# Attention transposes, key copies and mLSTM transposes moved, and the order of all queues made with a timeline simulation

## The chip, the cores and the metric

The kernel runs on one core of one Trainium2 chip. The metric is device time in microseconds (us) of one execution; the profile is of one execution on the same core. TensorE (PE) multiplies and transposes, VectorE (DVE) and ScalarE (ACT) do elementwise work, GpSimd (POOL) a small part of it, and SyncE (SP) issues nearly all transfers (DMA). Each engine works through a queue of its own, and engines wait for each other by semaphores.

## The reference

Two layers of an encoder are applied to 768 tokens: a sequence of 256 (token tiles 0 and 1, of 128 tokens each) and one of 512 (tiles 2 to 5). Weights are shared. All data is float32. Cut to what matters:

```
for l in range(2):
    aq, ak, av, lq, lk, lv, lo, lg = split(x @ w_in[l])
    att  = rmsnorm(diff_attention(aq, ak, av))        # 4 heads: softmax(s0) - lam * softmax(s1), with a distance bias
    h    = mlstm(lq, lk, lv, lg) + reversed mlstm     # 4 heads, in chunks of 128 tokens, states carried between them
    lstm = sigmoid(lo) * rmsnorm(h)
    x = layer_norm(ALPHA * x + concat(att, lstm) @ w_out[l])
    gate, up = split(x @ w_gu[l])                     # 2 x 2816 columns
    x = layer_norm(ALPHA * x + (gelu(conv3(gate)) * up) @ w_down[l])
```

## The kernel before

Every large product is made of three passes over float32r operands: a value is split into a high part and a rest (`wh` and `wl` for weights, the two halves of `actA` and `actB` for activations), and high x high, high x rest and rest x high are summed in PSUM. The class `Weights` loads each weight block by a DMA on SP into one of six `raw` buffers, and converts it: ACT writes `wh` (L171), DVE writes `wl` (L172). Twelve converted blocks may wait for use. For the FFN, DVE and POOL also form differences of blocks, T1 to T4 (L149), since the gate and up products are made by a scheme of seven products in place of eight.

A layer runs in these stages:

- The mLSTM's inputs and gates, and the values `av` and `lv` (`dense`, `lstm_in`, `gates`).
- Attention by heads: `att_in(h)` makes queries and keys (tiles aqkA, aqkB) and copies the keys into `sK` with their rest in `kL`; `att(h)` goes over the two sequences and their query tiles. For one query tile it makes two scores s (L728, L729), reduces them on DVE (L730), takes exponentials on ACT, combines the two halves on DVE (L737), transposes the result on PE (aT, L740), and multiplies with the values (u, L744). At a sequence's end `ao` is the normalised output, and PE transposes it (aoT, L757).
- The mLSTM by six chunks, `lstm_out(c)`: queries and keys are transposed (qkT, L592; copies into `qz` and `kt`), kq is their product (L615), DVE weighs it with the decay `pt` (L618) and the queries with `qet` (L622), PE makes the numerators num of four heads (L633, L636), and DVE and ACT divide and normalise them in `hq` (den, L643 to L656). `qet` has one buffer, and a DMA fills it for the next chunk (L602). `lo` (L345) is a dense product, its gate is applied to `hq`.
- W_out (tiles wo, L898), by two halves of the columns and six token tiles. In the second half each token tile is normalised (`layer_norm`, L845 to L857), sums S1 to S4 are formed on POOL or DVE (`combine`, L880 to L883), and PE transposes them (tiles y0T and y1T, L362), which ACT and DVE split into `actA` and `actB` (L364, L365).
- The FFN: 22 column tiles of seven products p (L942), and the down product dn by groups of three or four of these (L1002), added to `acc` on DVE (L1009).

Eight PSUM banks are shared by tags: three for d (dense tiles), two for s, one each for t, u and L. A tile that needs a bank waits until the tile before it in the bank was read.

The order in which the code is written isn't the order on the engines. `weave` mixes generators by shares, `prio` shifts the priority of what is issued inside it, and the framework's scheduler then sets the order of each engine's queue, by readiness in a simulation of its own and by priority. Only the order in each queue is fixed; on the chip an instruction at the head of a queue waits for its semaphores, and everything behind it waits with it. Chunks and heads meet in two lines:

```
weave((chain(att_in(1), att(1)), AT1, PR_A), (chain(lstm_states(lc), *[lstm_out(lc, c) for c in range(OUTS)]), 4 * OUTS + 9, PR_L), ...)
weave((chain(att_in(2), att(2)), AT2, PR_A), (chain(*[lstm_out(lc, c) for c in range(OUTS, NT)]), 4 * (NT - OUTS) + 1, PR_L), ...)
```

Names of tiles below carry numbers: s, aT and u have head, first token tile and query tile (s2200: head 2, sequence from tile 2, query tile 0, softmax half 0), kq and qkT the chunk, num chunk and head, lo and wo the token tile, raw, wh and wl the block.

## Time and profile before

| | us |
|---|---|
| Median of 3 runs | 1815.83 |
| Lowest and highest run | 1812.57 and 1816.02 |
| The profiled execution | 1814.85 |
| Its span, first to last instruction | 1813.1 |
| PE busy in the span | 1772.2 |
| DVE busy | 1348.4 |
| ACT busy | 774.3 |
| POOL busy | 244.4 |

An engine counts as busy while a record of it lasts. PE's matmuls overlap, so a busy PE may still wait for short times; how far apart matmuls start tells more. The granted clock of TensorE was 0.998 of full speed over the execution. The first matmul starts 7.3 us after the span's start, and the last 8.1 us are layer norm and output of the last token tile.

### The profile page before, as it was taken

To read this page: it belongs to the slowest core of one execution; us is meant where nothing else is said; L and a number is where in the kernel's file an instruction comes from. 1 tells how busy PE (TensorE), PEld (TensorE's weight loads), DVE (VectorE), ACT (ScalarE), POOL (GpSimd) and SP (SyncE) were. 2 spreads that over 40 slices of the span, in tenths; PEclk is the share of its full clock that TensorE was granted. 3 is DMA by queue.
4 is the path that set the end of the run, shared out by engine and by line. 5 is a ranking of instruction groups with operands and counts; after the bars stand their busy time and mean duration, and the time that the engine had idled before them with its cause. 6 is when DMAs were issued, how large, how long until landed. Compare 5 with 4: busy or idle time off the path is not lost. (4 is left out here: it accounts for less than half of the span.)

```text
span 1813.1 us, 26263 instructions
## 1 busy us (share of the span) xinstructions
PE 1772.2 (98%) x9692; PEld 1575.5 (87%) x9692; DVE 1348.4 (74%) x2592; ACT 774.3 (43%) x1636; POOL 244.4 (13%) x266
## 2 busy tenths in 40 slices
PE   8999999999999999999999999999999999999998
PEld 8877887889889889899898778878899898898996
DVE  4546887599877787787955468876997787787778
ACT  4445667144334334344233556671453343343340
POOL 2001011141111111110110011101411110111102
PEclk9999999999999999999999999999999999999999
DMA  5312221303122122123232123122122221221211
GB/s 190 100 53 71 76 60 59 139 24 95 57 82 82 47 82 73 56 69 96 94 97 80 53 64 94 47 86 107 37 87 70 65 82 51 78 82 47 82 65 70
DMA packets 89232, 138.09 MB, mean 76 GB/s; under 512 B 7792, under 2 KB 33008, under 8 KB 89104
## 3 DMA queue, kind: packets, MB, share of 16 engines
q1 hardware_dynamic: 88384, 136.05, 23.7%
q8 instruction: 76, 1.25, 0.3%
q14 instruction: 52, 0.43, 0.1%
q10 hardware_dynamic: 720, 0.37, 0.1%
HBM read 130.00 MB, written 6.39 MB: 75 GB/s over the span
## 5 line engine op out<-in xcount | busy, mean ns | idle before, releaser
L942 PE MATMUL p<-actA,wh 128*128 128x384 f32 x1408 | 363.5, 338 | 3.2 <-DVE g L967 3.2
L171 ACT ACTIVATE wh<-raw 128x512 fp32r<-128x512 f32 (+1 forms) x348 | 215.8, 631 | 275.3 <-PE p L942 110.1
L172 DVE TENSOR_TENSOR wl<-raw,wh 128x512 fp32r<-128x512 f32 (+1 forms) x348 | 244.0, 712 | 62.2 <-ACT wh L171 61.7
L942 PE MATMUL p<-actB,wh 128*128 128x384 f32 x1056 | 270.1, 337 | 0.0
L942 PEld LDWEIGHTS p<-actA,wh 128*128 128x128 f32 x1408 | 254.7, 188 | 5.8 <-DVE g L967 3.8
L942 PE MATMUL p<-actA,wl 128*128 128x384 f32 x704 | 237.3, 337 | 0.0
L149 POOL TENSOR_TENSOR T<-raw,raw 128x512 f32<-128x512 f32 x88 | 120.3, 1370 | 837.4 <-DVE wl L172 483.9
L1002 PE MATMUL dn<-wh,actB 128*128 128x512 f32 x576 | 209.1, 396 | 1.4 <-DVE acc L1009 1.4
L171 ACT ACTIVATE wh<-T 128x512 fp32r<-128x512 f32 x176 | 108.5, 629 | 220.6 <-DVE acc L1009 105.3
L942 PEld LDWEIGHTS p<-actB,wh 128*128 128x128 f32 x1056 | 191.2, 188 | 0.0
L1002 PE MATMUL dn<-wh,ring 128*128 128x512 f32 x480 | 179.2, 397 | 1.6 <-DVE acc L1009 1.6
L942 PE MATMUL p<-actB,wl 128*128 128x384 f32 x528 | 177.2, 336 | 0.0
L1009 DVE TENSOR_TENSOR acc<-acc,dn 128x512 f32<-128x512 f32 x144 | 98.3, 683 | 72.2 <-PE dn L1002 72.0
L172 DVE TENSOR_TENSOR wl<-T,wh 128x512 fp32r<-128x512 f32 x176 | 129.8, 749 | 22.1 <-ACT wh L171 22.0
L1002 PEld LDWEIGHTS dn<-wh,actB 128*128 128x128 f32 x576 | 108.0, 188 | 30.3 <-DVE acc L1009 3.4
L942 PEld LDWEIGHTS p<-actA,wl 128*128 128x128 f32 x704 | 132.2, 188 | 0.1
L898 PE MATMUL wo<-wh,actB 128*128 128x512 f32 x384 | 122.9, 397 | 0.0
L1002 PE MATMUL dn<-wl,actB 128*128 128x512 f32 x288 | 113.2, 393 | 0.0
L1002 PEld LDWEIGHTS dn<-wh,ring 128*128 128x128 f32 x480 | 90.0, 188 | 24.6 <-DVE acc L1009 4.2
L942 PEld LDWEIGHTS p<-actB,wl 128*128 128x128 f32 x528 | 99.1, 188 | 0.0
L1002 PE MATMUL dn<-wl,ring 128*128 128x512 f32 x240 | 94.7, 395 | 0.0
L898 PEld LDWEIGHTS wo<-wh,actB 128*128 128x128 f32 x384 | 71.8, 188 | 16.2
(270 smaller groups left out, 3387.9 us busy)
## 6 DMA issues: line engine op xcount, KB each, us to landing
raw<-in_w_g_dram SPq DMA_DIRECT2D x88, 256.0 KB, 2.8
raw<-in_w_u_dram SPq DMA_DIRECT2D x88, 256.0 KB, 2.6
raw<-in_w_down_dram SPq DMA_DIRECT2D x88, 256.0 KB, 2.7
raw<-in_w_out_dram SPq DMA_DIRECT2D x32, 256.0 KB, 2.7
pt<-scr_m SPq DMA_DIRECT2D x12, 512.0 KB, 3.9
qet<-scr_e SPq DMA_DIRECT2D x12, 512.0 KB, 5.2
raw<-in_w_c_dram SPq DMA_DIRECT2D x16, 264.0 KB, 4.0
raw<-in_w_av_dram SPq DMA_DIRECT2D x16, 256.0 KB, 3.5
```

Source lines behind the costliest of these rows:

```text
L149: src["engine"].tensor_tensor(out=src["tile"], in0=a, in1=b, op=ALU.subtract)
L171: self.nc.scalar.activation(h, v, AF.Identity)
L172: self.nc.vector.tensor_tensor(out=l, in0=v, in1=h.bitcast(F32), op=ALU.subtract)
L898: PE.matmul(p, actB[:, k, a, t * 128:(t + 1) * 128], units[k][1 + b], start=n + i == 0, stop=n == 7 and i == 2)
L942: PE.matmul(ps, blk[1 + a][:, k * 128:(k + 1) * 128], x[:, k, b, :], start=k + i == 0, stop=k == 3 and i == 2)
L1002: PE.matmul(p, x, (wh_, wl_)[b], start=k + i == 0, stop=k == nf - 1 and i == 2)
L1009: V.tensor_tensor(out=z, in0=z, in1=p, op=ALU.add)
```

## The change

Four edits by hand and one switch:

- aoT, the transposes of a head's output, become a function `finish` that is put into a list; the list is worked off by `finish_sequence` behind the next unit's scores, or behind the next head's key product.
- The key copies are issued in the order in which the scores read them, and with priority 60.
- `lstm_qk` for the next chunk is called behind the numerators of the chunk, no longer ahead of them.
- `PR_AO` goes, and the bank of u is taken later.
- `schedule_with_timeline_sim=True`: the framework's scheduler uses its timeline simulation when it orders the queues.

```
--- before.py
+++ after.py
@@ -52,7 +52,6 @@
 PR_S = -20
 PR_T = -20
 PR_E = 50
-PR_AO = -40
 PR_CONV1 = -100
 PR_CONV2 = -100
 SBUFS = 2
@@ -84,6 +83,7 @@
 WO_K = (4,5,0,1,6,7,2,3)
 WO_ORDER0 = (0, 1, 2, 3, 4, 5)
 NSG = 3
+PR_K = 60
 AT1 = 11
 AT2 = 8
 AT3 = 12
@@ -620,8 +620,6 @@
             dirs = [di for di in range(2) if (di, c) in cst]
             for di in dirs:
                 EN[E_QE].tensor_tensor(out=qet[:, di], in0=qz.rearrange("p h r j -> p r h j"), in1=qet[:, di], op=ALU.mult)
-            if c + 1 < NT:
-                lstm_qk(lc, c + 1)
             yield
             pns = {}
             for h in range(4):
@@ -649,6 +647,8 @@
                 S.activation(pt[:, 0, h, :], hs, AF.Square, accum_out=ssq[:, c, h:h + 1])
                 if h % 2:
                     yield
+            if c + 1 < NT:
+                lstm_qk(lc, c + 1)
             G.tensor_scalar(rsl[:, c], ssq[:, c], 128 * EPS, 1.0, op0=ALU.add, op1=ALU.mult)
             G.tensor_tensor(out=rsl[:, c], in0=rsl[:, c], in1=mhalf[:, 0:4], op=ALU.pow)
             for h in range(4):
@@ -692,6 +692,7 @@
                 pA = P("d", f"aqkA{h}{ui}")
                 pBu = pB[:, ui * 256:(ui + 1) * 256]
                 feat_major(uu, pA, pBu)
+                finish_sequence()
                 W.done(*uu)
                 for ps, tk in ((pBu, slice(0, SB)), (pA, slice(SB, T))):
                     if ui == 0:
@@ -700,14 +701,21 @@
                         V.scalar_tensor_tensor(out=sQ[hi_, 0, tk], in0=ps[lo_], scalar=qs, in1=sQ[lo_, 0, tk].bitcast(F32), op0=ALU.mult, op1=ALU.subtract)
                         V.scalar_tensor_tensor(out=sQ[lo_, 1, tk], in0=ps[hi_], scalar=qs, in1=sQ[hi_, 1, tk].bitcast(F32), op0=ALU.mult, op1=ALU.subtract)
                     else:
-                        S.copy(sK[lo_, 0, tk], ps[lo_])
-                        S.copy(sK[hi_, 1, tk], ps[hi_])
-                        S.copy(sK[hi_, 0, tk], ps[lo_])
-                        S.copy(sK[lo_, 1, tk], ps[hi_])
-                        V.tensor_tensor(out=kL[lo_, 0, tk], in0=ps[lo_], in1=sK[lo_, 0, tk].bitcast(F32), op=ALU.subtract)
-                        V.tensor_tensor(out=kL[hi_, 1, tk], in0=ps[hi_], in1=sK[hi_, 1, tk].bitcast(F32), op=ALU.subtract)
+                        with prio(PR_K):
+                            S.copy(sK[lo_, 0, tk], ps[lo_])
+                            V.tensor_tensor(out=kL[lo_, 0, tk], in0=ps[lo_], in1=sK[lo_, 0, tk].bitcast(F32), op=ALU.subtract)
+                            S.copy(sK[hi_, 0, tk], ps[lo_])
+                            S.copy(sK[hi_, 1, tk], ps[hi_])
+                            V.tensor_tensor(out=kL[hi_, 1, tk], in0=ps[hi_], in1=sK[hi_, 1, tk].bitcast(F32), op=ALU.subtract)
+                            S.copy(sK[lo_, 1, tk], ps[hi_])
                 yield
 
+
+        pending = []
+
+        def finish_sequence():
+            while pending:
+                pending.pop(0)()
 
         def att(h):
             slope = 2.0 ** (-8.0 * (h + 1) / 4)
@@ -715,7 +723,7 @@
                 nq = s1 - s0
                 n = nq * 128
                 keys = slice(s0 * 128, s1 * 128)
-                pu = P("u", f"u{h}{s0}")
+                pu = None
                 ssu = sm.tile([128, 4], F32, tag="ssu", name=f"ssu{h}{s0}")
                 sm0 = sm.tile([128, 4], F32, tag="sm0", name=f"sm0{h}{s0}")
                 for qt in range(nq):
@@ -735,6 +743,9 @@
                     V.reciprocal(cc, cc)
                     V.scalar_tensor_tensor(out=cc, in0=sm0[:, qt:qt + 1], scalar=nlam[:, l:l + 1], in1=cc, op0=ALU.mult, op1=ALU.mult)
                     V.scalar_tensor_tensor(out=tp[:, 0, :n], in0=tp[:, 1, :n], scalar=cc, in1=tp[:, 0, :n], op0=ALU.mult, op1=ALU.add)
+                    if pu is None:
+                        finish_sequence()
+                        pu = P("u", f"u{h}{s0}")
                     pa = P(TAG_AT[qt % 2], f"aT{h}{s0}{qt}")
                     for st in range(nq):
                         PE.transpose(pa[:, st * 128:(st + 1) * 128], tp[:, 0, st * 128:(st + 1) * 128], ident)
@@ -751,11 +762,14 @@
                 ao = ra.tile([128, 512], F32, tag="aT", name=f"ao{h}{s0}", bufs=2)
                 V.tensor_tensor(out=ao[:, :n].rearrange("p (a b) -> p a b", b=128), in0=pu[:, :n].rearrange("p (a b) -> p a b", b=128),
                                 in1=ssu[:, :nq].unsqueeze(2).to_broadcast([128, nq, 128]), op=ALU.mult)
-                pt_ = P(TAG_AOT, f"aoT{h}{s0}")
-                with prio(PR_AO):
+
+                def finish(h=h, s0=s0, s1=s1, nq=nq, n=n, ao=ao):
+                    pt_ = P(TAG_AOT, f"aoT{h}{s0}")
                     for qt in range(nq):
                         PE.transpose(pt_[:, qt * 128:(qt + 1) * 128], ao[:, qt * 128:(qt + 1) * 128], ident)
-                S.activation(av[:, s0:s1, h * 128:(h + 1) * 128], pt_[:, :n].rearrange("p (a b) -> p a b", b=128), AF.Identity, scale=again[:, l, h:h + 1])
+                    S.activation(av[:, s0:s1, h * 128:(h + 1) * 128], pt_[:, :n].rearrange("p (a b) -> p a b", b=128), AF.Identity, scale=again[:, l, h:h + 1])
+
+                pending.append(finish)
 
         def weave(*gens):
 
@@ -811,6 +825,7 @@
             next(lo, None)
 
         weave((chain(att_in(3), att(3)), AT3, PR_A), (split_lstm(), 13 - L1 - L2, PR_LO), (chain(*[split_att(h) for h in range(3)]), 4))
+        finish_sequence()
         weave((split_att(3), 1))
         RA.close()
 
@@ -1105,7 +1120,7 @@
     d["scr_m"] = nc.dram_tensor("scr_m", (DEPTH, 8, T), F32, kind="Internal").ap()
     d["scr_e"] = nc.dram_tensor("scr_e", (DEPTH, 8, T), F32, kind="Internal").ap()
     d["scr_x"] = nc.dram_tensor("scr_x", (T, D), F32, kind="Internal").ap()
-    with tile.TileContext(nc) as tc:
+    with tile.TileContext(nc, schedule_with_timeline_sim=True) as tc:
         with ExitStack() as ctx:
             trunk(ctx, nc, tc, d, o, depth)
     return nc
```

No instruction that computes is added or removed. What the order of the queues becomes is seen in the built programs. In each pair of excerpts the first is of the kernel before.

PE, in the mLSTM chunks of the first layer, from chunk 3's product kq3 on. The tiles lo2 are dense work.

```order
L615 MATMUL kq3_2386<-qz_1847,kt3_2185 128x128 x3
L744 MATMUL u20_2347<-av_227,aT200_2369 128x128 x2
L740 MATMUL aT201_2420<-ident_214,tp201_2404 128x128 x2
L728 MATMUL s2201_2536<-sK_229,sQ_228 128x512
L729 MATMUL s2201_2536<-kL_230,sQ_228 128x512
L345 MATMUL lo2_2693<-wh49_1462,actA_70 128x512
L345 MATMUL lo2_2693<-wl49_1463,actA_70 128x512
L345 MATMUL lo2_2693<-wh49_1462,actA_70 128x512
L345 MATMUL lo2_2693<-wh50_1468,actA_70 128x512
L345 MATMUL lo2_2693<-wl50_1469,actA_70 128x512
L345 MATMUL lo2_2693<-wh50_1468,actA_70 128x512
L345 MATMUL lo2_2693<-wh51_1474,actA_70 128x512
```

```order
L615 MATMUL kq3_2386<-qz_1847,kt3_2337 128x128 x4
L755 MATMUL u20_2365<-av_227,aT200_2369 128x128 x2
L751 MATMUL aT201_2411<-ident_214,tp201_2395 128x128 x2
L736 MATMUL s2210_2581<-sK_229,sQ_228 128x512
L737 MATMUL s2210_2581<-kL_230,sQ_228 128x512
L736 MATMUL s2211_2585<-sK_229,sQ_228 128x512
L737 MATMUL s2211_2585<-kL_230,sQ_228 128x512
L631 MATMUL num30_2419<-cst30_1665,qet3_2316 128x129
L631 MATMUL num30_2419<-cst31_1744,qet3_2316 128x129
L634 MATMUL num30_2419<-vaug_237,pt3_2084 128x129 x2
L755 MATMUL u20_2365<-av_227,aT201_2414 128x128 x2
L631 MATMUL num31_2420<-cst30_1665,qet3_2316 128x129
```

In the kernel before, ten more matmuls of lo2 and the transposes qkT4 follow before num30. In the changed one lo0 to lo4 stand ahead of these rows, num30 comes seven rows after kq3, and up to kq5 only the 24 matmuls of lo5 are dense work.

DVE, at the end of W_out in the first layer: layer norm of token tile 4 (`acc` with mva04 and rsa04), the splits of transposes into `actA` and `actB`, and conversions wl of FFN weights.

```order
L851 SCALAR_TENSOR_TENSOR acc_3376<-acc_3376,mva04_3800,lng_3386 128x1024
L365 TENSOR_TENSOR actB_2834<-y0T32_3829,actB_2834 128x4x128
L857 SCALAR_TENSOR_TENSOR acc_3376<-acc_3376,rsa04_3801,lnb_3387 128x1024
L365 TENSOR_TENSOR actB_2834<-y0T33_3836,actB_2834 128x4x128
L365 TENSOR_TENSOR actA_70<-y0T34_3843,actA_70 128x4x128
L172 TENSOR_TENSOR wl81_3948<-T4_81_3945,wh81_3947 128x512
L172 TENSOR_TENSOR wl82_3956<-T2_81_3943,wh82_3955 128x512
L901 SCALAR_TENSOR_TENSOR acc_3376<-acc_3376,wo15_3850 128x512
```

```order
L866 SCALAR_TENSOR_TENSOR acc_3376<-acc_3376,mva04_3800,lng_3386 128x1024
L172 TENSOR_TENSOR wl81_3948<-T4_81_3945,wh81_3947 128x512
L172 TENSOR_TENSOR wl82_3956<-T2_81_3943,wh82_3955 128x512
L172 TENSOR_TENSOR wl83_3962<-T3_83_3959,wh83_3961 128x512
L172 TENSOR_TENSOR wl84_3966<-T1_81_3941,wh84_3965 128x512
L872 SCALAR_TENSOR_TENSOR acc_3376<-acc_3376,rsa04_3801,lnb_3387 128x1024
L172 TENSOR_TENSOR wl85_3970<-raw82_3583,wh85_3969 128x512
L916 SCALAR_TENSOR_TENSOR acc_3376<-acc_3376,wo15_3850 128x512
```

Four conversions now stand between the two steps of the layer norm of tile 4, and the splits of y0T33 and y0T34 come behind the step that reads wo15.

POOL, at the same place: the sums S1 to S4 of token tile 4, the two small steps of the layer norm (rsa), and the differences T of FFN weights.

```order
L847 TENSOR_TENSOR rsa04_3801<-rsa04_3801,mhalf_71 128x1
L880 TENSOR_TENSOR S1_4_3807<-acc_3376 128x512
L882 TENSOR_TENSOR S3_4_3809<-acc_3376 128x512
L881 TENSOR_TENSOR S2_4_3808<-S1_4_3807,acc_3376 128x512
L883 TENSOR_TENSOR S4_4_3810<-acc_3376,S2_4_3808 128x512
L846 TENSOR_SCALAR rsa05_3878<-mva05_3877 128x1
L847 TENSOR_TENSOR rsa05_3878<-rsa05_3878,mhalf_71 128x1
```

```order
L862 TENSOR_TENSOR rsa04_3801<-rsa04_3801,mhalf_71 128x1
L149 TENSOR_TENSOR T3_88_3995<-raw84_3953,raw83_3951 128x512
L149 TENSOR_TENSOR T1_86_3973<-raw83_3951,raw79_3565 128x512
L895 TENSOR_TENSOR S1_4_3807<-acc_3376 128x512
L897 TENSOR_TENSOR S3_4_3809<-acc_3376 128x512
L896 TENSOR_TENSOR S2_4_3808<-S1_4_3807,acc_3376 128x512
L898 TENSOR_TENSOR S4_4_3810<-acc_3376,S2_4_3808 128x512
L861 TENSOR_SCALAR rsa05_3878<-mva05_3877 128x1
L862 TENSOR_TENSOR rsa05_3878<-rsa05_3878,mhalf_71 128x1
```

T3_88 and T1_86, which stood behind the layer norm of tile 5, now stand ahead of the sums of tile 4.

## Rows read from the trace of the kernel before

**Rows 1.** The page: busy us of each engine, share of the span, instructions.

```profile
PE 1772.2 (98%) x9692; PEld 1575.5 (87%) x9692; DVE 1348.4 (74%) x2592; ACT 774.3 (43%) x1636; POOL 244.4 (13%) x266
```

**Rows 2.** Stretches: length, busy us (count) of PE, PEld, DVE, ACT, POOL; PEclk, DMA.

```profile
105.00:186.00 81.00, 79.35 (x470) 63.43 (x470) 46.34 (x127) 42.78 (x118) 6.68 (x9) 1.00 0.14 44
186.00:312.00 126.00, 120.37 (x754) 102.75 (x753) 104.01 (x318) 89.73 (x271) 14.77 (x18) 1.00 0.20 60
312.00:366.00 54.00, 53.73 (x240) 43.35 (x239) 31.93 (x47) 10.32 (x19) 7.82 (x9) 1.00 0.40 140
366.00:402.00 36.00, 35.22 (x202) 30.11 (x201) 32.56 (x46) 14.13 (x25) 17.31 (x17) 1.00 0.01 3
402.00:905.00 503.00, 499.82 (x2603) 461.31 (x2602) 405.47 (x658) 191.91 (x315) 59.77 (x49) 1.00 0.24 77
```

**Rows 3.** Order of time, PE, two stretches: start, length, line, tiles.

```profile
218.25 0.28 PE L729 MATMUL s<-kL,sQ 128*128 128x256 f32 x1
218.37 0.28 PE L728 MATMUL s<-sK,sQ 128*128 128x256 f32 x1
...
223.36 0.61 PE L636 MATMUL num<-vaug,pt 128*128 128x129 f32 x4
223.81 0.39 PE L633 MATMUL num<-cst,qet 128*128 128x129 f32 x2
...
477.60 0.51 PE L942 MATMUL p<-actA,wh 128*128 128x384 f32 x2
...
479.18 0.52 PE L942 MATMUL p<-actA,wh 128*128 128x384 f32 x2
```

**Rows 4.** The chain that ended last: start, length, engine, tile, line, count.

```profile
1219.65 45.25 PE wo L898 x195
```

**Rows 5.** Waits of PE: for whom, us in total, times, longest.

```profile
PE aoT L757 <- DVE ao L752: 3.9, 6, 1.0
PE p L942 <- DVE g L967: 3.2, 2, 1.6
PE s L728 <- ACT sK L705: 3.2, 2, 1.6
PE dn L1002 <- DVE acc L1009: 3.0, 10, 0.6
PE qkT L592 <- DVE pt L618: 1.7, 2, 1.0
...
PE aoT L757 <- DVE cc L735: 1.6, 2, 0.8
```

**Rows 6.** Order of time, DVE, 393 to 395 us.

```profile
393.54 0.68 DVE L882 TENSOR_TENSOR S<-acc 128x512 f32<-128x512 f32 x1
394.14 0.68 DVE L881 TENSOR_TENSOR S<-S,acc 128x512 f32<-128x512 f32 x1
```

**Rows 7.** DVE's groups by form: busy us, mean ns of one, idle before.

```profile
L172 DVE TENSOR_TENSOR wl<-raw,wh 128x512 fp32r<-128x512 f32 x332 | 232.7, 711 | 55.8 <-ACT wh L171 55.3
...
L730 DVE CUSTOM_DVE_ANT_0 tp<-s,dneg 128x512 f32<-128x512 f32 x64 | 42.8, 684 | 9.4 <-PE s L729 9.3
...
L737 DVE SCALAR_TENSOR_TENSOR tp<-tp,cc 128x512 f32<-128x512 f32 x32 | 24.0, 749 | 0.4
...
L648 DVE SCALAR_TENSOR_TENSOR hq<-num,den,hq 128x128 f32<-128x128 f32 x48 | 15.7, 347 | 4.9 <-ACT hq L647 4.3
...
L643 DVE SCALAR_TENSOR_TENSOR den<-num,cols 128x2 f32<-128x2 f32 x48 | 6.9, 155 | 6.6 <-PE num L636 5.8
```

**Rows 8.** Waits of SP's DMA queue.

```profile
SPq L602 <- PE num L633: 62.6, 8, 10.7
```

**Rows 9.** The tile qet: who waited for it, and its DMA's landing.

```profile
  DVE qet L622: 5.4, 5
...
DMA to landing us min/median/max: 5.2/5.2/5.2
```

**Rows 10.** POOL's groups by form.

```profile
L149 POOL TENSOR_TENSOR T<-raw,raw 128x512 f32<-128x512 f32 x88 | 120.3, 1370 | 837.4 <-DVE wl L172 483.9 <-DMA raw<-in_w_u_dram 192.4 <-DVE g L967 87.1
```

More of the change, by code (lines that the diff above doesn't have):

```diff
@@ L54 @@
 PR_E = 50
-PR_AO = -40
 PR_CONV1 = -100
@@ L86 @@
 NSG = 3
+PR_K = 60
 AT1 = 11
@@ L651, in lstm_out @@
                     yield
+            if c + 1 < NT:
+                lstm_qk(lc, c + 1)
             G.tensor_scalar(rsl[:, c], ssq[:, c], 128 * EPS, 1.0, op0=ALU.add, op1=ALU.mult)
@@ L694, in att_in @@
                 feat_major(uu, pA, pBu)
+                finish_sequence()
                 W.done(*uu)
@@ L702, in att_in, with finish_sequence @@
                     else:
-                        S.copy(sK[lo_, 0, tk], ps[lo_])
-                        S.copy(sK[hi_, 1, tk], ps[hi_])
-                        S.copy(sK[hi_, 0, tk], ps[lo_])
-                        S.copy(sK[lo_, 1, tk], ps[hi_])
-                        V.tensor_tensor(out=kL[lo_, 0, tk], in0=ps[lo_], in1=sK[lo_, 0, tk].bitcast(F32), op=ALU.subtract)
-                        V.tensor_tensor(out=kL[hi_, 1, tk], in0=ps[hi_], in1=sK[hi_, 1, tk].bitcast(F32), op=ALU.subtract)
+                        with prio(PR_K):
+                            S.copy(sK[lo_, 0, tk], ps[lo_])
+                            V.tensor_tensor(out=kL[lo_, 0, tk], in0=ps[lo_], in1=sK[lo_, 0, tk].bitcast(F32), op=ALU.subtract)
+                            S.copy(sK[hi_, 0, tk], ps[lo_])
+                            S.copy(sK[hi_, 1, tk], ps[hi_])
+                            V.tensor_tensor(out=kL[hi_, 1, tk], in0=ps[hi_], in1=sK[hi_, 1, tk].bitcast(F32), op=ALU.subtract)
+                            S.copy(sK[lo_, 1, tk], ps[hi_])
                 yield
+        pending = []
+        def finish_sequence():
+            while pending:
+                pending.pop(0)()
         def att(h):
@@ L737, in att @@
                     V.scalar_tensor_tensor(out=tp[:, 0, :n], in0=tp[:, 1, :n], scalar=cc, in1=tp[:, 0, :n], op0=ALU.mult, op1=ALU.add)
+                    if pu is None:
+                        finish_sequence()
+                        pu = P("u", f"u{h}{s0}")
                     pa = P(TAG_AT[qt % 2], f"aT{h}{s0}{qt}")
@@ L753, in att, with finish @@
                                 in1=ssu[:, :nq].unsqueeze(2).to_broadcast([128, nq, 128]), op=ALU.mult)
-                pt_ = P(TAG_AOT, f"aoT{h}{s0}")
-                with prio(PR_AO):
+                def finish(h=h, s0=s0, s1=s1, nq=nq, n=n, ao=ao):
+                    pt_ = P(TAG_AOT, f"aoT{h}{s0}")
                     for qt in range(nq):
                         PE.transpose(pt_[:, qt * 128:(qt + 1) * 128], ao[:, qt * 128:(qt + 1) * 128], ident)
-                S.activation(av[:, s0:s1, h * 128:(h + 1) * 128], pt_[:, :n].rearrange("p (a b) -> p a b", b=128), AF.Identity, scale=again[:, l, h:h + 1])
+                    S.activation(av[:, s0:s1, h * 128:(h + 1) * 128], pt_[:, :n].rearrange("p (a b) -> p a b", b=128), AF.Identity, scale=again[:, l, h:h + 1])
+                pending.append(finish)
         def weave(*gens):
@@ L1107, in build @@
     d["scr_x"] = nc.dram_tensor("scr_x", (T, D), F32, kind="Internal").ap()
-    with tile.TileContext(nc) as tc:
+    with tile.TileContext(nc, schedule_with_timeline_sim=True) as tc:
         with ExitStack() as ctx:
```

5 lines of the change are left out of this document (2 added, 3 removed).

## The prediction

> **What bounds the kernel now.** I read the page's busy line first, then the stretches by stage, then TensorE's waits. PE is busy for 98% of the span [rows 1], so at first sight nothing is left but to issue fewer matmuls. The stretches [rows 2] correct that. They follow one layer: early attention (105 to 186 us), attention together with the mLSTM chunks (186 to 312), W_out (312 to 366), the way from W_out into the FFN (366 to 402), the FFN (402 to 905). PE stands idle 1.65, 5.63, 0.27, 0.78 and 3.18 us there. A busy record hides short waits, though: a record of 256 columns lasts 0.28 us, but the next one starts after 0.12; four records of 129 columns start in 0.45, and nine of 384 columns in 1.58 (from the one row to the other) [rows 3]. The 195 records of 512 columns in a row of W_out take 45.25 us, 0.232 each [rows 4]. By this spacing I price PE's work: 0.232 us for 512 columns, 0.1755 for 384, 0.12 for 256, and 0.111 for a record of 128 or 129 columns, where an f32 matmul is two records and a transpose one. Of the 754 records of 186 to 312 us [rows 2], 262 have 512 columns, 88 have 256 and the rest 128 or 129: 116 us of work in 126, so 10 us are lost, not 5.6. The same count gives 2.9 lost in 105 to 186, 2.1 in 366 to 402 and 4.4 in the FFN. That is 19 us in a layer, 39 in both: all that any order could win, outside the head and the tail.
>
> One rule of the Trainium skill would read this otherwise. In 312 to 366 us PE has 53.73 of 54 us busy while weight loads have 43.35 [rows 2]. The page Trainium Kernel Development and Optimization, section Performance Expectations, holds that matmul busy time is a bad measure and the busy share of weight loads a good one; by it a fifth of that stretch would be open. The spacing of [rows 4] comes from that very stage and is as tight as anywhere in the trace, so I give the order no such room.
>
> The second resource matters more. In 186 to 312 us DVE is busy 104.0 us of 126, against 46.3 of 81 in the stage before it [rows 2]. Between two chained steps PE is kept going by the dense tiles lo and aqk. They are the cover of this stage, and the order decides when they are used up.
>
> **The change part by part.**
>
> *The four edits by hand.* PE's waits say what they can win [rows 5]. The transposes of a head's output, aoT, wait 3.9 + 1.6 us, in eight places; the change issues them after the next unit's scores. The scores wait 3.2 us for the key copies; the change puts the copy that is read first in front. qkT waits 1.7 us; the change issues it behind the chunk's numerators. Together 10.4 us, both layers, if nothing takes their place. No instruction is added or removed, and no DMA.
>
> *The order.* The scheduler's new timing rearranges all five queues. Three places decide.
>
> First, the end of the mLSTM chunks. In the change, lo0 to lo4 and the last head's aqk tiles stand before chunk 2's numerators end; from there to the third loT, PE has 24 lo matmuls left and chained work otherwise. I add up both queues between num20's end and loT2. PE: 52 matmuls of 512 columns (12.1), 82 f32 matmuls (18.2) and 46 transposes (5.1) make 35.4 us. DVE must in the same stretch work through everything up to the split of loT1, since loT2 needs its bank: 171 instructions. Back to back, instructions start some 85 ns before the one ahead ends: 684 ns long, 0.60 apart [rows 6]. So I take durations [rows 7] less 85 ns: 42 instructions of some 512 elements at 0.60 (25.2), 8 conversions at 0.63 (5.0), 6 combinations of the two softmax halves at 0.66 (4.0), 32 steps on hq at 0.26 (8.4), 48 on den at 0.07 (3.5), and 39 small ones (4.4): 50.5 us. PE cannot reach loT2 in under 50.5, so it stands 15.1 us. In the kernel before, no such stretch has DVE ahead of PE, because the same DVE work is spread over some 15 us of PE work for each chunk.
>
> To this come the waits for qet. It has one buffer; its DMA waits for the last numerator of the chunk [rows 8] and takes 5.2 us to land [rows 9]. From num20's end, chunk 2's last reader of qet starts at about 2.4 (num22 and num23 wait for DVE to free their banks), so qet3 lands at about 7.8; DVE, at 3.9 by its queue, stands 4 us in front of it. Behind it in the queue stand chunk 2's hq steps, pt3 and the softmax of s221, and on PE num30 and the next scores wait for these. The same repeats at qet4 (4 us). At qet5 it is 0.6, its DMA standing on SP behind five weight loads that wait for DVE's conversions. Sum: 15.1 + 8.6 = 23.7 us per layer. As these waits have no row, the bounds are 15 (all covered) and 28 (ACT's waits add 4). I take 24, since the rows have both of its parts.
>
> Of the 12.9 us that the two attention stages lose now, I let 4 remain: 1.3 where num22 follows num20 at once, 1.5 at the last head's output, the rest in small steps. Attention: 24 + 4 - 12.9 = +15 per layer.
>
> Second, from W_out into the FFN. Between the last matmul of wo14 and y0T53 the change's DVE queue holds 28.3 us, PE's 21.0 (24 of wo15, 50 of p, 60 transposes). DVE's surplus is eight more weight conversions (0.65 each) and four differences T ahead of the splits that PE waits for. On POOL two T of 1.37 us [rows 10] now stand in front of the four sums of token tile 4, which the transposes y0T42 read; I add 1 us. So 8.3 us where 2.1 are lost now: +6.2, bounds +5 and +8.
>
> Third, the FFN. dn tiles and p products alternate in the change, which gives a dn bank some 2 us more to be emptied. PE's waits there are 3.0 us for acc and 3.2 for g [rows 5] in both layers; with what the records hide, I take 2.5 of 4.4 as won, bounds 1 and 4.
>
> Per layer: +15 + 6.2 - 2.5 = +19; both layers +38. The profiled execution took 1814.85 us, 1.75 over its span and 1 below the median of 1815.83. So 1814.85 + 38 = 1853 us.
>
> **The rivals.**
>
> *It is faster.* If the dense tiles still cover the chunks, the 10.4 us of the four edits and 2 x 2.5 us in the FFN come home: 1799 us. What decides is whether DVE's work between num20 and loT2 stays under PE's 35.4 us. By [rows 7] it would have to be 30% cheaper. For it: the edits do hit the waits that stand. Against it: the sums, which hold whatever the latencies are. 5%.
>
> *Only the throughput counts.* The qet waits vanish, since the chain reaches the stretch with DVE already late: 15 + 2 - 12.9 in attention, +5 at W_out, -4 in the FFN make +5 per layer, 1825 us. For it: 5.4 us of waits for qet in all are seen now [rows 9]. Against it: DVE waits 5 times even with 15 us for a chunk. 13%.
>
> *The clock falls.* The granted clock is 1.00 in each stretch of [rows 2], while PE never idles over 5%. In the change it works 35 of some 59 us. Were it set to 1.2 GHz, the 35.4 us would take 71 and set the pace in place of DVE: 12 us more per layer, 1877 us. The page TensorE: Matmul & The Clock Gate, Part 1, states that an array which idles is put from 2.4 to 1.2 GHz; no row here shows idling inside the kernel that does it. 7%.
>
> *The change doesn't do what it says.* It does: aoT, qkT and the key copies stand where they should; what is open is only the pace. With all shifts hidden the time is within 0.2%. 3%.
>
> **How the numbers follow.** Forecast 1853, own range 1840 to 1864, 60%; waits of ACT on top, 1864 to 1874, 12%; only throughput 13%; clock 7%; faster 5%; same 3%. From 1825 to 1870 some 80% lies: the lower end is the bare queue sums; the upper end takes attention's 28, W_out's +8 and the FFN's 1 in place of 24, 6.2 and 2.5, 7 us per layer more, and stands a little over this sum's 1867. A measurement of this kernel can tell about 0.2% from no change. Faster 5%, same 3%, slower 92%.
>
> **What would show it.** In the profile after, PE's idle time should gather in some 55 to 60 us of each layer, from chunk 2 to loT2, with DVE near 85% or more busy there; PE's longest waits should be for DVE at kq, num and s, and DVE should wait for the qet DMA at each chunk. Early attention should lose less than the 1.65 us of idle time now; aoT and sK should go from the list of waits. In the 40 us before the FFN, PE should wait for DVE's splits. If PE is idle less than 8 us in that attention stretch, the queue sums are wrong; if the loss lies in the FFN or the head, so is the place.

## The result: 5% slower

The changed kernel takes 1905.47 us (median of 4 runs, 1903.12 to 1909.25) against 1814.95 for the kernel before in the same comparison: ratio 1.0503, 95% interval 1.0481 to 1.0524. The forecast was 1853, its range 1825 to 1870: slower was right, the size was not. The change costs 91 us where 38 were forecast.

From the page of the changed kernel, busy us of each engine, and the granted clock in 40 slices:

```profile
PE 1810.1 (95%) x9692; PEld 1620.9 (85%) x9692; DVE 1359.4 (71%) x2592; ACT 780.7 (41%) x1636; POOL 241.9 (13%) x266
...
PEclk9999988898999999999999999888999999999999
```

PE's busy time rose by 38 us over [rows 1] with the same 9692 instructions. A matmul that counts as busy for longer is held up or slower, and the last line shows one reason: in both layers the granted clock, 1.00 everywhere in [rows 2], falls. The stretches of the first layer, columns as in [rows 2]:

```profile
100.00:186.00 86.00, 86.00 (x494) 72.66 (x494) 46.51 (x121) 42.98 (x116) 5.19 (x7) 1.00 0.20 62
...
256.00:272.00 16.00, 13.21 (x59) 11.30 (x60) 10.56 (x38) 5.91 (x21) 1.20 (x2) 0.58 0.22 67
272.00:330.00 58.00, 42.86 (x226) 36.29 (x225) 47.90 (x142) 39.62 (x118) 7.84 (x10) 0.83 0.21 64
330.00:380.00 50.00, 42.10 (x200) 33.47 (x200) 19.85 (x51) 12.53 (x38) 1.94 (x2) 0.89 0.23 84
...
410.00:450.00 40.00, 31.44 (x166) 27.14 (x164) 37.52 (x51) 16.29 (x29) 19.24 (x17) 0.88 0.15 50
...
475.00:955.00 480.00, 479.68 (x2496) 444.07 (x2495) 379.46 (x617) 179.31 (x292) 53.16 (x47) 1.00 0.24 75
```

Early attention and the FFN are denser than before. The chunks (256 to 330), the last head with the start of W_out (330 to 380) and the way into the FFN (410 to 450) are not, and each of the three has a lower clock.

What half the clock costs is seen in W_out, where equal products of 512 columns follow each other. Two stretches of it, columns as in [rows 2], and PE in order of time from each of them (start, length, line, tiles, count):

```profile
364.00:371.00 7.00, 6.44 (x16) 4.56 (x15) 3.94 (x6) 0.00 (x0) 0.00 (x0) 0.50 1.01 398
373.00:379.00 6.00, 6.00 (x28) 4.84 (x27) 1.38 (x2) 0.00 (x0) 0.00 (x0) 1.00 0.27 107
```

```profile
364.39 0.63 PE L913 MATMUL wo<-wh,actB 128*128 128x512 f32 x1
364.82 0.63 PE L913 MATMUL wo<-wl,actB 128*128 128x512 f32 x1
365.25 1.05 PE L913 MATMUL wo<-wh,actB 128*128 128x512 f32 x2
...
374.58 0.63 PE L913 MATMUL wo<-wh,actB 128*128 128x512 f32 x2
375.05 0.39 PE L913 MATMUL wo<-wl,actB 128*128 128x512 f32 x1
375.28 0.62 PE L913 MATMUL wo<-wh,actB 128*128 128x512 f32 x2
```

At a granted 0.50 (1.2 GHz) 512 columns take 0.43 us from start to start, at 1.00 (2.4 GHz) 0.23, as in [rows 4].

So lost time has two parts now. I take the time from each matmul's start to the next, less the spacings that the prediction uses. Of what is left over, as much as the matmul itself grows by at the granted clock is put down to the clock, the rest to waits. This is an accounting: in a chain, slower matmuls also make others wait, and how the two split there can shift by some us with no change in time. Sums of both layers, waits + clock, in us (the last column takes in the stretches that the others leave out):

| kernel | time over before, us (95%) | first scores to num20 | num20 to loT2 | loT2 to wo05 | wo14 to p1_2 | FFN to dn600 | all |
|---|---|---|---|---|---|---|---|
| before | | 10.5 + 0 | 9.6 + 0 | 7.6 + 0 | 8.8 + 0 | 9.2 + 0 | 50.7 + 0 |
| changed | 91 (87 to 95) | 6.5 + 0.9 | 50.4 + 20.8 | 19.7 + 10.4 | 20.4 + 8.2 | 3.0 + 0 | 103.4 + 40.3 |
| switch_alone | 95 (92 to 98) | 6.7 + 0 | 56.8 + 13.3 | 19.4 + 8.7 | 20.5 + 10.0 | 3.0 + 0 | 109.7 + 32.0 |
| edits_alone | 2 (0 to 4) | 10.2 + 0 | 11.3 + 0 | 9.1 + 0 | 8.8 + 0 | 8.6 + 0 | 52.8 + 0 |
| dense_held | 72 (69 to 75) | 24.8 + 8.5 | 26.5 + 0 | 13.7 + 10.7 | 20.7 + 9.8 | 3.0 + 0 | 91.3 + 29.0 |
| dense_spread | 64 (59 to 68) | 16.9 + 1.3 | 31.6 + 11.5 | 11.3 + 3.9 | 20.3 + 9.3 | 3.0 + 0 | 87.1 + 26.1 |
| dense_fine | 64 (60 to 68) | 26.2 + 4.9 | 27.0 + 1.0 | 15.8 + 6.9 | 20.5 + 7.7 | 3.0 + 0 | 96.0 + 20.4 |
| pe_timeline | 104 (101 to 107) | 15.0 + 4.2 | 57.3 + 16.7 | 20.0 + 7.3 | 12.1 + 4.1 | 4.0 + 0 | 116.3 + 32.3 |
| pe_before | 85 (82 to 88) | 35.6 + 4.4 | 21.5 + 4.2 | 12.4 + 7.2 | 19.5 + 7.7 | 12.3 + 0 | 111.4 + 25.6 |
| pe_dve_before | 23 (21 to 26) | 14.4 + 0 | 13.6 + 1.5 | 8.2 + 3.1 | 8.3 + 0 | 14.7 + 2.9 | 65.0 + 7.5 |
| ffn_entry | 85 (82 to 88) | 5.9 + 1.7 | 48.9 + 16.8 | 19.8 + 10.4 | 11.2 + 0 | 15.0 + 2.7 | 104.0 + 31.6 |
| ffn_order | -5 (-7 to -3) | 11.6 + 0 | 8.7 + 0 | 7.5 + 0 | 8.8 + 0 | 3.1 + 0 | 44.3 + 0 |

(The second column is the ratio less one, times 1814 us.) The changed kernel's 53 us more of waits and 40 of clock make the 94 us by which its span is longer. Its longest waits of PE, to be held against [rows 5]:

```profile
PE aoT L769 <- DVE ao L763: 12.4, 8, 2.5
PE y0T L362 <- DVE actB L365: 8.2, 2, 5.2
PE y1T L362 <- DVE actB L365: 7.6, 2, 5.0
PE qkT L592 <- DVE hq L646: 7.5, 5, 3.2
...
PE kq L615 <- DVE qz L597: 6.6, 5, 2.2
PE wo L913 <- ACT actB L364: 6.2, 2, 3.1
...
PE dn L1017 <- DVE acc L1024: 0.6, 2, 0.3
```

The waits of s for sK and of p for g are gone, those of dn fell from 3.0; aoT, which the edits were aimed at, waits over twice as long as before (12.4 us for 3.9 + 1.6).

### The profile page after: what moved, and what is told of

Its sections match the earlier page's. It is cut to its first block, busy times and chain, and to the rows that moved or that the text cites. A ratio compares the mean times of both kernels' runs of the same rounds, so it can differ in the third digit from the quotient of the medians.

```text
span 1907.5 us, 26347 instructions
## 1 busy us (share of the span) xinstructions
PE 1810.1 (95%) x9692; PEld 1620.9 (85%) x9692; DVE 1359.4 (71%) x2592; ACT 780.7 (41%) x1636; POOL 241.9 (13%) x266
## 5 line engine op out<-in xcount | busy, mean ns | idle before, releaser
L172 DVE TENSOR_TENSOR wl<-raw,wh 128x512 fp32r<-128x512 f32 (+1 forms) x348 | 242.3, 704 | 87.1 <-ACT wh L171 69.7
L957 PEld LDWEIGHTS p<-actA,wh 128*128 128x128 f32 x1408 | 258.8, 190 | 5.6 <-ACT actA L364 0.9
L913 PE MATMUL wo<-wh,actB 128*128 128x512 f32 x384 | 130.8, 418 | 9.2 <-ACT actB L364 6.2
L172 DVE TENSOR_TENSOR wl<-T,wh 128x512 fp32r<-128x512 f32 x176 | 117.5, 683 | 4.3 <-ACT wh L171 4.2
L913 PEld LDWEIGHTS wo<-wh,actB 128*128 128x128 f32 x384 | 75.7, 199 | 28.6 <-ACT actB L364 6.6
```

Source lines behind the costliest of these rows:

```text
L172: self.nc.vector.tensor_tensor(out=l, in0=v, in1=h.bitcast(F32), op=ALU.subtract)
L913: PE.matmul(p, actB[:, k, a, t * 128:(t + 1) * 128], units[k][1 + b], start=n + i == 0, stop=n == 7 and i == 2)
L957: PE.matmul(ps, blk[1 + a][:, k * 128:(k + 1) * 128], x[:, k, b, :], start=k + i == 0, stop=k == 3 and i == 2)
```

## The experiments

**Which part of the change.** switch_alone is the kernel before with the new timing, edits_alone the changed kernel without it:

```
-    with tile.TileContext(nc) as tc:
+    with tile.TileContext(nc, schedule_with_timeline_sim=True) as tc:
```

> The kernel before with the timeline simulation switched on and none of the four edits. Theory A (the new order of the queues does the damage, since it uses up the dense tiles ahead of the mLSTM chunks): 1895 to 1915 us, with the granted clock below 1.00 from chunk 2 on, as in the changed kernel. Theory B (the edits do it: transposes that come late make the chain longer): 1810 to 1830 us.

> The four edits with the scheduler of before. Theory A: 1800 to 1813 us, the 10.4 us of waits that the edits aim at come home in part, clock 1.00 throughout. Theory B: above 1860 us.

Measured: 1909.59 us, ratio 1.0525 (1.0508 to 1.0543), and 1816.83 us, 1.0011 (1.0001 to 1.0020). The switch is the whole loss. The edits win none of the 10.4 us that they aimed at: with the scheduler of before aoT still waits 5.6 us, s for sK 2.8; qkT no longer waits, but num now waits 2.8 us and kq 1.4.

**Is it the missing cover?** Three kernels keep the switch and the edits, and tie dense tiles behind steps of the chain (a tie sets the order of issue on PE, no more). First by whole tiles:

```
+PIN = {"lo2": "kq2", "aqk30": "kq3", "aqk31": "kq4", "lo3": "s320", "lo4": "s322", "lo5": "s300"}
...
-                tok_major(t, units, p, slice(0, 512))
+                with behind(f"{tag}{t}"):
+                    tok_major(t, units, p, slice(0, 512))
```

> The changed kernel, with five dense tiles tied behind steps of the chain (lo2 behind kq2, the queries of head 3 behind kq3, its keys behind kq4, lo3 to lo5 behind scores of head 3), so that PE has dense work at each chunk again. Nothing else is told to the scheduler. Theory A (the cover is what is missing): between num20 and the end of wo05 most of the 49 us that a layer loses there come back, all but some 12, and the clock stays at 1.00 there; 1830 us (1820 to 1850). The loss of some 11 us per layer between wo14 and the FFN stays. Rival (the chain itself became slow by the new order on DVE, whatever PE does beside it): above 1880 us.

> As dense_held, but all dense tiles from chunk 1 on are tied, so that none is spent early: lo0 and the keys of head 2 behind kq1, lo1 behind kq2, lo2 behind kq3, queries and keys of head 3 behind kq4 and kq5, lo3 to lo5 behind scores of head 3. In dense_held the loss between num20 and loT2 fell, but chunk 1, now bare, lost 9 us more. Theory (a loss appears wherever the chain runs without dense work): from the first scores to wo05 a layer loses some 20 us in place of 53, the clock stays at 1.00 there; 1840 us (1830 to 1855). Rival (the new order on DVE and ACT makes the chain slow, with or without dense work beside it): 35 us or more are lost there, above 1865 us.

In dense_fine a tile is cut into quarters:

```
+    "lo1": ("kq2", "num21", "num23", "qkT3"),
+    "lo2": ("kq3", "num31", "num33", "qkT4"),
...
+                with behind(name, k // 2):
+                    PE.matmul(ps, xh(k, t, a), (h, l)[b][:, cols], start=k + i == 0, stop=k == 7 and i == 2)
```

> As dense_spread, but each dense tile is cut into four pieces of 6 or 12 matmuls, tied behind four steps of its chunk in turn (kq, the first two num, the last two num, the next qkT), and lo3 to lo5 behind scores and u of head 3. In dense_spread a tile stood as one block behind kq, and PE waited at num, qkT and kq, where nothing dense was left; 36 to 41 us were lost in a layer from the first scores to wo05 (13 in the kernel before). Theory (each dependent pair of the chain needs a piece of dense work between): some 22 us are lost there, 1843 us (1835 to 1855). Rival (it matters only how much dense work a chunk has, the rest is the order on DVE and ACT): 1868 to 1880 us.

Measured: 1887.08 us (1.0397, 1.0382 to 1.0413), 1876.94 (1.0352, 1.0328 to 1.0376) and 1880.09 (1.0355, 1.0333 to 1.0376). All three are far from what the theory said; dense_held and dense_spread lie in their rivals' ranges, and dense_fine at the upper end of its own. Where the dense work was put, it did what it should: from num20 to loT2 dense_fine loses 28 us in place of 71, only 1.0 of it by the clock, and from num30 to num40 each layer waits 2.2 us where the changed kernel waits 6.3 and 5.9 and the kernel before 1.6 and 2.3. But the loss came up elsewhere: from the first scores to num20 it is 31 us, in place of 7 in the changed kernel. Keys that are tied late now make scores wait (3.2 us in [rows 5]), those of head 2 for 6.8 us in both layers and those of head 3, after the chunks, for 8.7:

```profile
PE s L752 <- ACT sK L723: 15.5, 6, 4.4
```

Cover matters, then, but it did not bring the kernel near the old time, and the ties can't tell whether that is the ties or the rest of the order.

**Which queue.** The code and all instructions are those of the kernel before. One function ties PE's queue, instruction by instruction, into a given order, and the scheduler arranges the others around it:

```
+def in_order(nc, tc):
...
+    for item in PE_ORDER.split(";"):
+        name, *k = item.split()
+        for _ in range(int(k[0]) if k else 1):
+            n = seen[name] = seen.get(name, -1) + 1
+            i = by[name, n]
+            if prev is not None:
+                tc.add_manual_dep(i, prev.name, mybir.DependencyInfo(mybir.DependencyClass.NoSync, mybir.DependencyReason.DATA), reason="order")
+            prev = i
```

> The code of the kernel before, timeline simulation on, but PE's queue is tied, instruction by instruction, into the order that it has in the kernel before; DVE, ACT, POOL and SP are ordered by the simulation around it. Theory (the place of the dense work in PE's queue makes the loss): the waits of PE stay near the 51 us of the kernel before, the clock at 1.00: 1812 to 1835 us. Rival (the order that the simulation gives to DVE and ACT makes the loss): 1865 us or more.

> The opposite: the code of the kernel before and its scheduler, but PE's queue is tied into the order that the timeline simulation gave it in switch_alone; the other queues are ordered by the scheduler of before around it. Theory (PE's order makes the loss): 1885 to 1915 us, with a lower clock from chunk 2 on. Rival (the other queues make it): 1815 to 1850 us.

> As pe_before, but DVE's queue too is tied into its order in the kernel before; only ACT, POOL and SP are ordered by the timeline simulation. If the simulation's order on DVE made the loss of pe_before (84 us): 1812 to 1830 us, clock 1.00. If ACT or POOL make it: 1865 us or more; in between, both do.

Measured: pe_before 1897.84 us (1.0468, 1.0452 to 1.0484), pe_timeline 1917.11 (1.0573, 1.0555 to 1.0591), pe_dve_before 1837.98 (1.0129, 1.0114 to 1.0144). By the time alone each side makes nearly the whole loss: PE's new order with the old scheduler around it, and PE's old order with the simulation around it. By place they differ. The loss from num20 to loT2 goes with PE's order: 74 us in pe_timeline and 26 in pe_before, where switch_alone loses 70 and the kernel before 10. The loss from wo14 to p1_2 goes mostly with the other queues: 27 us in pe_before and 16 in pe_timeline, where switch_alone loses 31 and the kernel before 9. And up to num20 pe_before loses 40 us, where switch_alone loses 7: this is a cost of the mixture, which the simulation's own order doesn't have. In both kernels the queues that aren't tied were arranged anew around the tie, so neither holds DVE's queue of switch_alone or of the kernel before. In pe_before it is mostly DVE: with DVE tied as well, some 60 of the 84 us are gone. The waits of pe_before show where the queues off PE are late:

```profile
PE aoT L758 <- DVE ao L753: 13.7, 8, 3.1
...
PE y1T L363 <- POOL S L883: 4.8, 1, 4.8
PE y0T L363 <- POOL S L883: 4.8, 1, 4.8
```

Ahead of ao on DVE stand weight conversions or steps of the chunks, and ahead of the sums S on POOL a difference T, as in the changed kernel's order ahead of the prediction. Of the 23 us that stay in pe_dve_before the largest part is in the FFN (17.6 lost there, 9.2 before); attention up to wo05 makes 13 more. Whether ACT, POOL or SP makes them wasn't tried.

**DVE's two terms in the chunks.** qet_once fills qet once in a layer; lighter_dve drops two DVE steps:

```
+            if "qet" in kts:
+                qets[c] = kts["qet"]
+                return
```

```
+                if c < 2:
                     EN[E_TRI].tensor_tensor(out=pt[:, di], ...
...
-            for h in range(4):
+            for h in range(4 if c < 2 else 0):
```

> The changed kernel, without the transfers that fill qet for chunks 1 to 5 (the buffer is filled once in a layer, so the later chunks compute with wrong weights). By the prediction's step DVE stands 8.6 us in a layer for these transfers, so some 17 us go: 1888 us. By the trace of the changed kernel, where DVE waits 4.0 us for them in both layers together, 0 to 4 us go: 1901 to 1906 us.

> The changed kernel, without two DVE steps in chunks 2 to 5: the mask added to the decay and the last scaling of hq (the output is not the reference's). In each chunk these are 1.28 and 1.14 us of DVE work on which PE does not wait at once; some 7 us of them lie between num20 and loT2. By the prediction's term (DVE, back to back, sets the pace from num20 to loT2) 7 us per layer go: 1891 us (1888 to 1895). If the loss is the length of the chain, PE to DVE to ACT to PE, with DVE idle in between (it is busy 56 of 70 us there), at most 2 us per layer go: 1901 to 1906 us.

Measured: 1905.98 us (1.0510, 1.0495 to 1.0526), the time of the changed kernel; and 1893.44 (1.0435, 1.0420 to 1.0451), 12 us less. So the transfers of qet cost nothing. The trace had said so, in what DVE sat idle for ahead of qet:

```profile
  DVE hq L646: 10.5, 9
...
  DMA qet<-scr_e: 4.0, 5
```

DVE's own work does cost: 6 us a layer came, where the prediction's term has 7. But the place is not the one of the term. By the sums of the table, about 5 of the 12 us came ahead of num20; from num20 to loT2 the waits fell by only 1 to 2 us in both layers (49 in place of 50.4), and the clock's part by some 6 (14 in place of 20.8). DVE was busy only 58.5 of 74 us from 256 to 330 in the changed kernel. So the time speaks for the term, and the waits in the stretch speak against DVE setting the pace there; that what is taken off DVE is taken off a chain through PE, ACT and DVE would fit both, but isn't shown. (In lighter_dve some matmuls of lo5 also moved a few places ahead.)

**Into the FFN.** The conversions for the FFN are tied behind DVE's splits and POOL's sums of a token tile:

```
-        W.done(*units)
+        with tc.issue_after(marks["split"].ins), tc.issue_after(marks["sum", G].ins):
+            W.done(*units)
```

> The changed kernel, with the weight conversions and differences for the FFN tied behind the splits and sums of token tile 4; attention keeps its order. If the conversions ahead of the splits are the cause of the stop between wo14 and the FFN (15 us lost in a layer there, 4.4 before), 8 to 11 us per layer come back: 1885 us (1882 to 1892), and the granted clock in these 40 us is 1.00. If DVE simply has more to do there than PE, whatever comes first, the FFN's first products wait in its place: 1900 us or more.

> dense_spread, and the conversions for the FFN tied behind the splits of token tile 3 (the same point as tile 2's in the queue), later than in the changed kernel and earlier than in ffn_entry. If the way into the FFN only needs the conversions between the splits, as the kernel before has them, it loses 5 to 7 us from wo14 to p1_2 and no more than 3 after it, and the time is 8 to 14 us under dense_spread; if DVE lacks the time, the loss moves behind p1_2 as in ffn_entry, and 0 to 5 us are won.

> dense_fine with the tie of spread_entry on the FFN's conversions. spread_entry was 1.3 us under dense_spread, as the loss moved behind p1_2. The same is expected here: 0 to 5 us under dense_fine. If nothing but these two places loses time in the changed kernel, this one comes within 20 us of the kernel before; what is left is the price of the order itself.

Measured: 1900.69 us (1.0468, 1.0452 to 1.0484), 1875.63 (1.0341, 1.0325 to 1.0356) and 1870.19 (1.0311, 1.0294 to 1.0329). In ffn_entry the stop between wo14 and p1_2 went (28.6 lost, now 11.2, clock 1.00), and its clock with it. A new one came behind it, at the FFN's first products:

```profile
PE p L959 <- DVE u L980: 11.8, 2, 5.9
```

So 17 us came back and 15 were lost again: put behind the splits as a block, the conversions hold up DVE's first steps of the FFN instead. The tie in the middle shares the loss between both places (20.3 and 8.6 in spread_entry). In fine_entry the tie won 10 us over dense_fine, more than the 0 to 5 expected. It is the fastest kernel with the switch and the edits, and still 56 us above the kernel before, not within 20.

**The clock.** filled puts useless products ahead of num, entry_filled into two waits on the way into the FFN:

```
+                        if c >= 2:
+                            for _ in range(6):
+                                PE.matmul(pn[:, 385:512], ident, ident[:, 0:127], start=True, stop=True, skip_group_check=True)
```

```
+                    pd = P("s", f"fillA{l}")
+                    with tc.issue_after(mm.ins):
+                        for i in range(6):
+                            last = PE.matmul(pd, ident, ln["g"][:, 0:512], start=True, stop=True)
```

> The changed kernel with useless work: ahead of each num tile of chunks 2 to 5 six f32 products of 127 columns into a part of the bank that nobody reads, 96 of them in a layer, 21.5 us at full clock. The other instructions keep nearly the order of the changed kernel. Theory (the lower clock costs what its rows show, some 10 us in a layer from num20 to loT2): the useless work lies in PE's waits, the clock stays at 1.00 there, and the kernel gets no slower, though 43 us of work are added: 1890 to 1903 us. Rival (the clock falls only where PE would wait anyway and costs nothing): 1906 to 1925 us.

> The changed kernel with useless work in two waits between wo14 and the FFN: six f32 products of 512 columns behind the last matmul of wo15, where PE waits 5.5 us in the changed kernel, and three near y0T52, where it waits 3.2 us; 7.7 us per layer at full clock, into a free bank. After each of these waits the granted clock is 0.50 for 6.8 us in the changed kernel. Theory (PE's idling lowers the clock, and the lower clock costs 3.5 to 4.7 us per layer there): the clock stays at 1.00, and more work takes less time: 1896 to 1901 us. Rival (the clock falls for another cause, or its cost is hidden): 1904 to 1912 us.

Measured: 1922.19 us (1.0598, 1.0582 to 1.0613) and 1907.89 (1.0517, 1.0499 to 1.0534). Both lie in the rivals' ranges, not in the theory's. In filled 43 us of added work cost 17: from num20 to loT2 the clock's part fell from 20.8 to 5.6 us, the waits' only from 50.4 to 43.0. That the products stood in the chain itself, and so made others wait, would explain it, but wasn't tested; that the lower clock costs time in the chunks is not shown by this run. In entry_filled the first wait was filled in full and the clock stayed up behind it: the 15.4 us of added work cost no time that the intervals tell, and 19.3 us are lost there in place of 28.6. But DVE's order changed too, and a wait came back one step later, with a fall of the clock behind it. PE there, and the same place in the changed kernel:

```profile
422.92 0.47 PE L913 MATMUL wo<-wh,actB 128*128 128x512 f32 x1
428.62 1.94 PE L362 MATMUL y0T<-ident,acc 128*128 128x128 f32 x8 [5.24 <-DVE actB L365]
430.40 0.69 PE L957 MATMUL p<-actA,wh 128*128 128x384 f32 x1
```

```profile
420.09 5.31 PE L919 MATMUL fillA<-lng,ident 128*128 128x512 f32 x12
425.50 1.23 PE L362 MATMUL y0T<-ident,acc 128*128 128x128 f32 x8
426.58 0.66 PE L362 MATMUL y0T<-ident,S 128*128 128x128 f32 x4
431.05 1.50 PE L968 MATMUL p<-actA,wh 128*128 128x384 f32 x3 [3.81 <-ACT actA L364]
```

(The first fence is of the changed kernel.) Eight transposes last 1.94 us behind the wait, and 1.23 behind the useless work. To see the clock without a chain, single_stops puts waits into the FFN of the kernel before, with PE's order tied:

```
+            if (l, f) in STOPS:
+                st = ft.tile([128, HALF], F32, tag="stop", name=f"stop{l}{f}", bufs=1)
+                S.copy(st, p1)
+                for _ in range(STOPS[l, f] - 1):
+                    S.copy(st, st)
+                PE.matmul(p2[:, 0:128], ident, st[:, 0:128], start=True, stop=True)
             product(p2, A12)
```

> The kernel before, its order on PE tied, with eight stops of PE in the FFN, four in a layer: between p1 and p2 of column tiles 4, 9, 14 and 18 a small useless product waits for 1, 4, 8 and 14 copies of 384 columns on ACT in the first layer, for 2, 6, 11 and 24 in the second. With some 0.36 us a copy and 0.5 us for the way there and back the stops are about 0.9, 1.9, 3.4, 5.5 and 1.2, 2.7, 4.5, 9.1 us long, 29 us together. Theory (a long wait of PE is followed by a stretch at 0.50 granted clock, which costs by itself): the clock falls right behind the longer ones and nowhere else, each fall costs 1.7 to 3.4 us more than the stop, and the time is 1850 to 1862 us. Rival (the clock falls for a reason of the attention stage, not for a single wait): 1.00 throughout, 1840 to 1847 us.

Measured: 1884.11 us (1.0388, 1.0371 to 1.0406). A copy takes over 0.5 us, not 0.36 (twelve in a row take 6.48), and ACT does other work in between, so the stops came out at 1.5, 4.7, 6.4 and 10.1 us in the first layer and 2.1, 5.7, 7.9 and 15.5 in the second, 54 us in place of 29; the expected time was made for the shorter ones. Behind the stops of 1.5 and 2.1 us the granted clock stays at 1.00; behind the six others it is 0.50. PE at the second stop of the first layer and the first of the second:

```profile
583.74 0.80 PE L963 MATMUL p<-stop,ident 128*128 128x128 f32 x2 [4.53 <-ACT stop L962]
...
584.98 0.52 PE L944 MATMUL p<-actA,wl 128*128 128x384 f32 x1
585.30 0.84 PE L944 MATMUL p<-actA,wh 128*128 128x384 f32 x2
...
588.59 0.33 PE L944 MATMUL p<-actA,wl 128*128 128x384 f32 x1
588.77 0.51 PE L944 MATMUL p<-actA,wh 128*128 128x384 f32 x2
```

```profile
1409.26 0.49 PE L963 MATMUL p<-stop,ident 128*128 128x128 f32 x2 [1.90 <-ACT stop L962]
...
1409.93 0.33 PE L944 MATMUL p<-actA,wl 128*128 128x384 f32 x1
1410.10 0.51 PE L944 MATMUL p<-actA,wh 128*128 128x384 f32 x2
```

Nowhere else in this kernel's stages does the clock fall. The stops add 54 us of waits to the FFN, and the clock 11, just under 2 for each of the six falls: dense work behind a long wait pays a second time. The theory's mechanism holds, here in dense work.

**A version that beats both.** ffn_order is the kernel before with PE's queue tied: its own order, but from p1_2 to the last dn5 that of switch_alone.

> The kernel before, but from the first p1_2 of a layer to its last down product of the sixth group PE's queue is tied into the order of switch_alone, where dn tiles and p products alternate; the rest of PE's queue is that of before. If PE's order alone gives the 3 us per layer that the changed kernel wins in the FFN (1.5 us lost there in place of 4.7): 1808.5 us (1806 to 1811). If it needs the other queues too: 1814 us or more.

Measured: 1808.55 us, ratio 0.9973 (0.9961 to 0.9984). The waits of dn for acc are gone from the list, and the FFN loses 3.1 us in both layers in place of 9.2. One thing that the simulation did better is the alternation of dn and p on PE, and that can be had alone. (It also loses less from the first scores to num20, 7 us for 10.5; that wasn't tried alone.)

## Why the prediction was wrong

- **What bounds the kernel**: held, as far as it was tested. PE's work at the prediction's spacings is the same in all kernels of the table, so their lost times must differ as their spans do; what the spacings give is where the time was lost.
- **The four edits, up to 10.4 us**: nothing came (edits_alone). In the changed kernel aoT was forecast to go from the list of waits, and heads it. The step named who waited, not why: DVE is late with ao, and a transpose issued later waits for the same DVE queue.
- **num20 to loT2, 24 us of waits in a layer**: 25.2 came, in the place foretold; that the size fits so well is luck. Its part for qet, 8.6, was nothing, and DVE was far from back to back: busy 79% from 256 to 330 us, not 85. (The counts of DVE's instructions there add up to 175, not to 171; the 50.5 us are the sum of the list as it stands.) I take what stood in place of qet's part to be the way of the chain from PE to ACT and DVE and back, which a sum over single queues doesn't hold; no run shows this.
- **The rest of attention, 4 us in a layer**: this term was too small. From loT2 to wo05 alone 9.9 us of waits came, 3.8 before. I gave the last head's output 1.5 us. Its cover, lo5, is used up in the chunks, and the matmuls of wo that stand there instead need `actB`, and wait for it themselves (6.2 us in both layers, in the list above).
- **Into the FFN, 6.2 us more in a layer**: 5.8 more of waits came (10.2 for 4.4 from wo14 to p1_2), with the mechanism as told, conversions ahead of the splits. ffn_entry shows that the wait goes with them, and that moving all of them only moves it. The sum priced DVE's steps as if POOL stood still; two of them are slower there beside its differences T (last section).
- **The FFN, 2.5 us won in a layer**: 3.1 won, and ffn_order shows that PE's order alone does it.
- **The clock, put at 7% and 12 us in a layer**: this is the step that failed. It came, with 20 us in a layer, in all three places where PE waits and not in the chunks alone. I made it a rival to the sum, where it is a term of it: an order that makes PE wait several us at a time, as mine did by its own sums (4 us at a qet, 8 in front of the FFN), pays it in addition. The Trainium skill says as much in TensorE: Matmul & The Clock Gate, HAM oscillation — how this bites in real kernels: waits between stretches of work can put the array back to the lower clock again and again. single_stops agrees, with 6 falls behind 6 waits of 4.7 us and more. It shows for dense work that a fall costs time of its own; for the chunks, 10 us in a layer, this rests on the accounting.

Waits in excess of the forecast (53 in place of 38) and the clock (40 in place of 0) make 55 us; the miss is 52, as the profiled execution lies 4 us above the median. The cause named for the chunks, dense work used up early on PE, is borne out by place: their loss comes with PE's order and the old scheduler (pe_timeline) and is a good third of it with PE's old order (pe_before). The loss in front of the FFN comes mostly with the order off PE, where the prediction had put it on DVE.

## What to carry to other kernels

When a new order makes TensorE wait, add up the waits first, and then the clock as a term of its own: half the speed in the stretch behind a long wait, priced from rows at 0.50. An order of queues is one thing made of five; PE's queue of one schedule with the others arranged by another was about as slow as the bad schedule, and partly in new places. So tie one queue at a time, compare by place and not only by time, and take over only the piece that a tie shows to win. Removing a wait wins only what isn't lost again at the next late step: in ffn_entry 17 us came back in one place and 15 went in the next.

## What the runs showed of the hardware

- A single wait of PE of 4.7 us in a dense stage is followed by a granted clock of 0.50 until 4.6 us behind it (from 583.7 to 588.3 us in single_stops); waits of 1.5 and 2.1 us leave it at 1.00. Six falls cost just under 2 us each on top of the waits.
- DVE's step on 128x1024 elements in SBUF takes longer while POOL works. In the kernel before, whose POOL runs the differences T later, and in the changed one (line, operation, tiles, form, count, busy us, mean ns, idle before):

```profile
L857 DVE SCALAR_TENSOR_TENSOR acc<-acc,rsa,lnb 128x1024 f32<-128x1024 f32 x12 | 15.4, 1281 | 7.3 <-POOL rsa L847 7.1
```

```profile
L872 DVE SCALAR_TENSOR_TENSOR acc<-acc,rsa,lnb 128x1024 f32<-128x1024 f32 x12 | 18.7, 1561 | 7.4 <-POOL rsa L862 6.8 <-DVE acc L866 0.5
```

In the changed kernel eight of the twelve take 1.28 us, with no POOL work beside them. The other four, two in a layer, take 1.92 to 2.32, all beside a T on POOL. The first of them, the conversion behind it, and POOL at that time:

```profile
423.32 2.29 DVE L872 SCALAR_TENSOR_TENSOR acc<-acc,rsa,lnb 128x1024 f32<-128x1024 f32 x1
425.53 1.75 DVE L172 TENSOR_TENSOR wl<-raw,wh 128x512 fp32r<-128x512 f32 x1
```

```profile
422.88 3.85 POOL L149 TENSOR_TENSOR T<-raw,raw 128x512 f32<-128x512 f32 x2 [3.32 <-DVE wl L172]
```

Such a conversion takes 0.69 us with no POOL work beside it. So these two steps, which stand ahead of the split that PE waits 5.24 us for in front of the FFN, are some 2 us longer by POOL's work (an estimate: 2.29 + 1.75 less 1.28 + 0.69). The Trainium skill has this in SBUF — State Buffer, SBUF: two separate sides: DVE steps with two inputs in SBUF and POOL's share a pair of ports that one of them holds at a time. The trace agrees for this step; DVE's splits, which read PSUM, take 0.67 us beside POOL's work and 0.68 without.
